# Attention's first loads, the fillers' weight loads and the last modulation load in another order

## The chip, the core and the metric

The kernel runs on one core of a Trainium2 chip. The time is the device time of one execution in microseconds (us), the median of several runs. The core has five engines with an instruction queue each: TensorE (PE) for matmuls, VectorE (DVE) and ScalarE (ACT) for elementwise work, GpSimd (POOL), and SyncE (SP), which here only issues DMAs. Each engine takes its instructions in the order in which they were written out. "Granted clock" is the share of TensorE's full clock that the chip's throttle allowed, as the profile records it.

## The reference

One layer of a Griffin-style block on x of 1024 tokens x 1024 channels, float32:

```python
sh1, sc1, g1, sh2, sc2, g2 = split(silu(c) @ ada_w + ada_b)       # six modulation vectors
h = rmsnorm(x, ln1_g) * (1.0 + sc1) + sh1
q, k, v, cb, cc, cx, ga, gb = split(h @ w_in)
q = rmsnorm(q, q_norm_g); k = rmsnorm(k, k_norm_g)                # 16 heads of 64
y_a = stick_breaking_attention(q, k, v)
y_b = cb * causal_dwconv(cc * cx, conv_w)                         # 3 taps
merged = sigmoid(ga) * (y_a @ w_branch_a) + sigmoid(gb) * (y_b @ w_branch_b)
x = x + g1 * (merged @ w_out)
h = rmsnorm(x, ln2_g) * (1.0 + sc2) + sh2
x = x + g2 * ((silu(h @ w_ffn_gate) * (h @ w_ffn_up)) @ w_ffn_down)
```

Stick-breaking attention weighs key s for query t > s by sigmoid(z_ts) times the product of (1 - sigmoid(z_tj)) over the keys j between them; there is no softmax.

## The kernel before

Matmuls run in a reduced float32 format at full rate, so every operand is split into a high and a low part (`whi`, `wlo`, `ath`, `atl`, `ya`'s two halves and so on): ACT copies the high part, DVE subtracts it from the original to get the low part, and three matmuls (high x high, high x low, low x high) make one product. The stages in order: modulation and norm, the projections, attention, branch a with its gates, W_out with the residual, the FFN.

**Attention** (`attention()`, from about 577 to 995 us in the trace) runs 16 heads x 8 query blocks of 128 queries, 128 steps. A step is: scores `z` on PE (L913, L914), sigmoid into `pt` on ACT (L915), the running product along the keys as one scan on DVE (L923; block i scans (i+1) x 128 elements), transposes `tr` on PE (L936, two steps later), the high copy `ath` on ACT (L939), the low part `atl` on DVE (L940), and every second step the product with the values, `o` on PE (L951, L952). Then ACT writes `otmp` (L956), DVE adds to `oy` (L958), and SP stores it to `d_ya` (L960). The scan form needs differences of neighbouring values: head pairs load `va` and `vb` (the values and the values one row on, 512 KB each, `load_v`, L844), `att_dv(h, 0)` subtracts them on DVE, and `att_dv(h, 1)` splits the difference into `vt` (ACT L855, DVE L136). L136 is the line of a helper that many DVE operations share. `att_load(h)` loads a head's q (`sqt`) and k (`skh`, `skl`), six DMAs on SP (L833 to L835).

**Fillers.** PE's own work in attention is less than that of DVE, so `fillers()` yields matmuls of other branches between attention's: for each of 8 column blocks m and two token halves n, cb = h @ w_cb (L1012 to L1014, into one of two `pj` banks), multiplied with a loaded tile of the convolution (`cy`, L1024, product L1030), split (`ybh` L1033, `ybl` L1034) and stored; later the same with w_b, and the gate product `mb` (L1062). The weight tile of an m is one load `raw<-w_cg` (L505) of 512 KB, split by ACT (L516) and DVE. n = 0 reads the h that is still in place; the first four k blocks of n = 1 have been stored to `d_h` and come back by two loads of 1 MB, hi and lo, into `big` (L1092). HEAD = 16 filler pieces are written out ahead of the first attention step.

**Branch a** loads attention's result back (`yr<-d_ya`, L1160, two buffers), splits it into `ya` (ACT L1164, DVE L136) and multiplies by w_a in the last heads and behind them; the gate's products `sgi` are L1184 (which frees PE's bank), L1185, L1190. Beside it `mods_last()` computes the last modulation vectors: it loads the raw c row broadcast to 128 partitions (`cab`, 512 KB, on POOL's queue, L1127), applies Silu (ACT L1128), and `mod_sums` loads 16 pieces of ada_w (`ad`, 512 KB each, three buffers, POOL's queue, L636) and reduces each with cab on DVE (L637).

**What sets the order.** The code is written in one order, and a scheduler places the instructions on each engine by its own estimate of times and by priority. `tc.issue_after(x)` holds the instructions written inside it until x has been placed, so that they don't move ahead of it; it adds no semaphore by itself. `lastld[0]` is the latest value load, `lastz[0]` the latest score matmul, `lastav[0]` the latest value product. DMAs of SP and ACT use eight semaphores in rotation, so a DMA issue also waits for the DMA that had its semaphore before.

Of the kernel before, what the change touches and what calls it, by code (L numbers as in the profile page):

```python
# [9 lines left out]
F32 = mybir.dt.float32  # L10
F32R = mybir.dt.float32r
AF = mybir.ActivationFunctionType
ALU = mybir.AluOpType
# [4 lines left out]
P = 128  # L18
T = 1024
D = 1024  # L20
KT = D // P
H = 16
DH = 64
# [7 lines left out]
def block_kernel(tc, x, x_t, cols, ada_1, ada_2, ada_row, w_q, w_kv, w_cg, w_a, w_b, w_o, w_g, w_u, w_d, out):  # L31
    nc = tc.nc
# [144 lines left out]
    cab = sp.tile([P, D], F32, name="cab")  # L177
# [648 lines left out]
    def att_load(h):  # L826
        pr, e0 = h // 2, (h % 2) * DH
        sqt = bp.tile([P, T], F32R, tag="sq", bufs=2, name=nm("sqt"))
        skh = bp.tile([P, T], F32R, tag="skh", bufs=2, name=nm("skh"))
        skl = bp.tile([P, T], F32R, tag="skl", bufs=2, name=nm("skl"))  # L830
        for e in range(2):
            es = slice(e * DH, (e + 1) * DH)
            nc.sync.dma_start(sqt[es].bitcast(F32), d_q[e][pr, e0:e0 + DH, :])  # L833
            nc.sync.dma_start(skh[es].rearrange("p (i t) -> p i t", t=P).bitcast(F32), d_k[0][pr // 4][:, e0:e0 + DH, pr % 4].rearrange("i p t -> p i t"))
            nc.sync.dma_start(skl[es].rearrange("p (i t) -> p i t", t=P).bitcast(F32), d_k[1][pr // 4][:, e0:e0 + DH, pr % 4].rearrange("i p t -> p i t"))  # L835
        hd[h] = (sqt, skh, skl)

    def load_v(h, e):
# [52 lines left out]
    lastav = [None]  # L891
    lastz = [None]
    lastld = [None]
    npt = [0]
    ats = {}
    ptof = {}
# [70 lines left out]
    def attention():  # L967

        steps = [(h, i) for h in range(H) for i in (LAST if h == H - 1 else ORDER)]
        for s in range(len(steps) + DAV):  # L970
            flush[0] = s >= len(steps)
            if s < len(steps):
                h, i = steps[s]
                if s % 8 == (0 if h else 3) and h + 1 < H:
                    with tc.issue_after(lastld[0].ins):
                        att_load(h + 1)
                with tc.issue_after(lastz[0].ins) if s else ExitStack():
                    if s in (1, 2):
                        att_dv(0, s - 1)
                    if s % 8 in ((4, 6) if h % 2 else (3, 5)) and h + 1 < H:  # L980
                        att_dv(h + 1, s % 8 // 5)
                    if s % 16 in (6, 7) and s + 16 < len(steps):
                        load_v(2 * (s // 16) + 2, 7 - s % 16)
                if s == 54:
                    with tc.issue_after(lastld[0].ins):
                        vl = load_vlast(1)
                if s == 56:
                    turn_vlast(1, vl)
                yield from att_scores(h, i)
            tr_ = att_trans(*steps[s - 2]) if 0 <= s - 2 < len(steps) else iter(())  # L990
            av_ = att_av(steps[s - DAV][0], steps[s - DAV][1] // 2) if s >= DAV and s % 2 != DAV % 2 else iter(())
            yield from itertools.islice(tr_, 1)
            if s >= DAV and steps[s - DAV][1] == 5:
                yield from av_
            yield from tr_
            if s < len(steps):
                att_scan(*steps[s])
            yield from av_

    def ps_f():  # L1000
# [15 lines left out]
    def fillers():  # L1016
        cb_w = {}
        for m, n in [(m + d, n) for m in range(0, KT, 2) for n in range(2) for d in range(2)]:
            if n == 0:
                with tc.issue_after(lastld[0].ins) if m > 1 else ExitStack():  # L1020
                    cb_w[m] = load_ch(w_cg[0, m])
            w = cb_w[m]
            y = fp.tile([P, 512], F32, tag="st", bufs=3, name=nm("cy"))
            nc.sync.dma_start(y, d_y[m, :, n * 512:(n + 1) * 512])  # L1024
            ps = ps_f()
            for kk in range(0, KT, KQ):
                if kk:
                    yield 0.65 * KQ
                mm_ch(ps, w, hh[n], hl[n], kk, kk + KQ)
            nc.vector.tensor_tensor(out=y, in0=ps, in1=y, op=ALU.mult)  # L1030
            yh = fq.tile([P, 512], F32R, tag="ybh", bufs=2, name=nm("ybh"))
            yl = fq.tile([P, 512], F32R, tag="ybl", bufs=2, name=nm("ybl"))
            nc.scalar.activation(yh, y, AF.Copy)  # L1033
            nc.vector.tensor_tensor(out=yl, in0=y, in1=yh.bitcast(F32), op=ALU.subtract)  # L1034
            nc.sync.dma_start(d_yb[0][n][:, m, :], yh.bitcast(F32))
            nc.sync.dma_start(d_yb[1][n][:, m, :], yl.bitcast(F32))
            yield 0.65 * KQ
        def load_sb(m, n):
            sb = fp.tile([P, 512], F32, tag="sgi", bufs=2, name=nm("sgi"))
            nc.sync.dma_start(sb, d_sgb[m, :, n * 512:(n + 1) * 512])  # L1040
            return sb

        sbs = [load_sb(m, 0) for m in range(2)]
        yh, yl = [], []
        for n in range(2):
            yh.append(big())
            yl.append(big())
            for k in range(0, KT, 2):
                nc.sync.dma_start(yh[n][:, k:k + 2].bitcast(F32), d_yb[0][n][:, k:k + 2])
                nc.sync.dma_start(yl[n][:, k:k + 2].bitcast(F32), d_yb[1][n][:, k:k + 2])  # L1050
        wb = {}
        for m, n in [(0, 0), (1, 0), (0, 1), (1, 1)] + [(m, n) for m in range(2, KT) for n in range(2)]:
            if n == 0:
                wb[m] = load_ch(w_b[m])
            sb = sbs.pop(0) if sbs else load_sb(m, n)
            ps = ps_f()
            for kk in range(0, KT, KQ):
                if kk:
                    yield 0.65 * KQ
                mm_ch(ps, wb[m], yh[n], yl[n], kk, kk + KQ)  # L1060
            mb = fp.tile([P, 512], F32, tag="st", bufs=3, name=nm("mb"))
            nc.vector.tensor_tensor(out=mb, in0=ps, in1=sb, op=ALU.mult)  # L1062
            nc.sync.dma_start(d_mb[m, :, n * 512:(n + 1) * 512], mb)
            yield 0.65 * KQ
# [16 lines left out]

    with tc.high_priority():
        att_load(0)
        for j in range(HEAD):
            next(fl)
            if j == 1:
                vl = load_vlast(0)
                turn_vlast(0, vl)
                load_v(0, 1)
                load_v(0, 0)  # L1090
                for e in range(2):
                    nc.sync.dma_start((hh, hl)[e][1][:, :4].bitcast(F32), d_h[e])  # L1092
    at_ = attention()
    flush, nfl = [0], 0
    pe, mine = len(nc.cur_bb.bb.instructions), set()
# [27 lines left out]
    def mods_last():  # L1123

        cab = mlp.tile([P, D], F32, name="cab3")
        with tc.issue_after(lastav[0].ins):
            nc.gpsimd.dma_start(cab, ada_row[0:1, :].broadcast_to([P, D]))  # L1127
            nc.scalar.activation(cab, cab, AF.Silu)  # L1128
        yield
        yield from mod_sums((3, 5), lambda i: mlp.tile([P, D], F32, tag="ad", bufs=3, name=nm("ad")),  # L1130
                            lambda s, t_: mlp.tile(s, F32, tag=t_, bufs=1, name=nm(t_)), cab, nc.gpsimd,
# [600 lines left out]
```

## Time and profile before

| | us |
|---|---|
| median of 3 runs (lowest, highest) | 1819.37 (1817.88, 1820.55) |
| the profiled execution's own time | 1820.9 |
| its span, first to last instruction | 1819.1 |
| PE busy | 1793.0 (99%) |
| DVE, ACT, POOL busy | 1358.5, 807.5, 369.8 |
| mean granted clock | 0.994 |

How to read the lines of the profile: in a timeline row stand the start, the duration, the engine, the line, the operation, output<-inputs, the shapes, how many instructions were merged (x2), and in brackets how long the engine had been idle ahead of it and what ended that wait. SPq is SP's queue; its rows are issues of DMAs, not their transfers. In the waits view the three numbers are the total, the number of waits and the longest. In the windows view stand, behind the window's length, each engine's busy time, then the granted clock, the share of the DMA engines and the rate in GB/s. PE is busy in nearly all of the span, so an engine that is late shows as a short PE wait.

### The profile page before, as it was taken

Reading aid. Unit: us, or ns where it says so; the run is one execution under the profiler, and the core shown is the slowest. Engines: PE = TensorE matmul, PEld = TensorE weight load, DVE = VectorE, ACT = ScalarE, POOL = GpSimd, SP = SyncE. Lnnn points to the kernel's source line nnn. Section 1 sums busy time; section 2 is a strip of 40 time slices with the busy share of each in tenths; the row PEclk is TensorE's granted clock in tenths of the full one; section 3 lists DMA queues with packets and bytes.
Section 4 is the critical chain, followed back from the end, with each engine's and each line's share of the span. In section 5 each row is a group of like instructions: output and inputs, shape, how many; then the busy total and the mean of one; then the engine's idle time right before and its main releaser. Section 6 shows DMA issues by size and latency. Waiting matters only on the chain.

```text
span 1819.1 us, 24498 instructions
## 1 busy us (share of the span) xinstructions
PE 1793.0 (99%) x8599; PEld 1490.5 (82%) x8599; DVE 1358.5 (75%) x1980; ACT 807.5 (44%) x1509; POOL 369.8 (20%) x297
## 2 busy tenths in 40 slices
PE   8999999999999999999999999999999999999999
PEld 6888877888888788888887888877888888878887
DVE  5876586787774789999996764689877887644766
ACT  5534364333433567666674221754443444322321
POOL 0024234733331000000000100115434444200000
PEclk9999999999999999999999999999999999999999
DMA  9479654223545977796645866424443443299876
GB/s 381 160 240 384 239 171 139 87 99 118 206 141 168 260 184 209 218 306 165 171 130 164 283 207 205 134 90 181 163 151 139 151 178 147 112 355 326 283 228 224
DMA packets 165006, 359.06 MB, mean 197 GB/s; under 512 B 15538, under 2 KB 60938, under 8 KB 163732
## 3 DMA queue, kind: packets, MB, share of 16 engines
q1 hardware_dynamic: 128300, 289.65, 48.9%
q10 hardware_dynamic: 33096, 55.25, 8.5%
q0 software_dynamic: 3488, 12.59, 2.0%
q8 instruction: 69, 1.13, 0.3%
q14 instruction: 53, 0.43, 0.1%
HBM read 247.84 MB, written 109.62 MB: 197 GB/s over the span
## 4 chain that ended last, share of the span: by engine, by line
PE 84%; DVE 6%; DMA 5%; ACT 2%; issue 2%; SPq 0%; ACTq 0%; POOL 0%; DVEq 0%; POOLq 0%
PE pj L293 9%; PE pj L133 7%; PE pj L131 7%; PE pj L132 7%; PE e L131 7%; PE e L132 7%; PE e L133 6%; PE e L1560 4%; PE e L1561 4%; PE e L1562 4%; PE pj L1012 4%; PE pj L1013 4%; PE pj L1014 4%; PE tr L936 3%; PE o L952 2%; PE z L913 2%
## 5 line engine op out<-in xcount | busy, mean ns | idle before, releaser
L923 DVE TENSOR_TENSOR_SCAN pt<-pt,mk 128x128 f32<-128x128 f32 (+7 forms) x128 | 172.4, 1347 | 0.7 <-ACT pt L915 0.7
L131 PE MATMUL e<-big,whi 128*128 128x512 f32 x352 | 138.0, 392 | 2.1 <-ACT c L1460 2.0
L132 PE MATMUL e<-big,whi 128*128 128x512 f32 x352 | 137.7, 391 | 0.0
L293 PE MATMUL pj<-whi,big 128*128 128x512 f32 x448 | 133.8, 396 | 3.9 <-ACT big L262 3.9
L133 PE MATMUL e<-big,wlo 128*128 128x512 f32 x352 | 137.5, 391 | 0.0
L136 DVE TENSOR_TENSOR c<-e,c 128x512 f32<-128x512 f32 x138 | 92.9, 687 | 57.0 <-PE e L133 55.9
L136 DVE TENSOR_TENSOR c<-pj,c 128x512 f32<-128x512 f32 x140 | 93.2, 682 | 45.5 <-PE pj L133 45.2
L131 PE MATMUL pj<-big,whi 128*128 128x512 f32 x320 | 125.0, 391 | 0.0
L133 PE MATMUL pj<-big,wlo 128*128 128x512 f32 x320 | 124.8, 390 | 0.0
L132 PE MATMUL pj<-big,whi 128*128 128x512 f32 x320 | 124.6, 389 | 0.0
L1560 PE MATMUL e<-whi,f 128*128 128x512 f32 (+1 forms) x319 | 121.8, 382 | 1.5 <-DMA f<-d_f 1.5
L1561 PE MATMUL e<-wlo,f 128*128 128x512 f32 (+1 forms) x319 | 121.8, 382 | 0.0
L1562 PE MATMUL e<-whi,f 128*128 128x512 f32 (+1 forms) x319 | 121.6, 382 | 0.0
L915 ACT ACTIVATE pt<-z,rq 128x512 f32<-128x512 f32 (+1 forms) x192 | 105.2, 576 | 23.3 <-PE z L914 22.8
L1012 PE MATMUL pj<-big,whi 128*128 128x512 f32 x256 | 114.3, 447 | 0.0
L136 POOL TENSOR_TENSOR ws<-raw,raw 128x512 f32<-128x512 f32 x40 | 54.5, 1362 | 275.8 <-DMA raw<-w_cg 127.7
L940 DVE TENSOR_TENSOR atl<-tr,ath 128x512 fp32r<-128x512 f32 (+1 forms) x192 | 102.8, 549 | 9.7 <-ACT ath L939 7.9
L939 ACT ACTIVATE ath<-tr 128x512 fp32r<-128x512 f32 (+1 forms) x192 | 93.1, 488 | 29.8 <-PE tr L936 28.9
L132 PE MATMUL e<-rl,whi 128*128 128x512 f32 x264 | 103.6, 392 | 2.5 <-DVE rl L136 2.5
L131 PE MATMUL e<-rh,whi 128*128 128x512 f32 x264 | 103.3, 391 | 0.2 <-ACT rh L1238 0.2
L133 PE MATMUL e<-rh,wlo 128*128 128x512 f32 x264 | 103.4, 392 | 0.0
L293 PEld LDWEIGHTS pj<-whi,big 128*128 128x128 f32 x448 | 84.9, 190 | 22.3 <-ACT big L262 4.7
(288 smaller groups left out, 4771.9 us busy)
## 6 DMA issues: line engine op xcount, KB each, us to landing
f<-d_f SPq DMA_DIRECT2D x77, 512.0 KB, 4.8
d_f<-fs SPq DMA_DIRECT2D x70, 512.0 KB, 3.6
raw<-w_cg SPq DMA_DIRECT2D x40, 512.0 KB, 4.2
raw<-w_u SPq DMA_DIRECT2D x26, 512.0 KB, 3.2
raw<-w_g SPq DMA_DIRECT2D x25, 512.0 KB, 3.6
raw<-w_kv SPq DMA_DIRECT2D x20, 512.0 KB, 5.9
ld<-ada SPq DMA_DIRECT2D x16, 512.0 KB, 7.0
d_t<-ts SPq DMA_DIRECT2D x16, 512.0 KB, 6.7
```

The lines of the kernel that those rows point to most:

```text
L131: nc.tensor.matmul(ps, wh[:, k, :], fh[:, k, :], start=(k == 0), stop=False)
L132: nc.tensor.matmul(ps, wh[:, k, :], fl[:, k, :], start=False, stop=False)
L133: nc.tensor.matmul(ps, wl[:, k, :], fh[:, k, :], start=False, stop=(k == 3))
L136: eng.tensor_tensor(out=out, in0=a, in1=b, op=op)
L293: nc.tensor.matmul(ps, a, b, start=(k == 0 and q == 0), stop=(k == KT - 1 and q == 2))
L915: nc.scalar.activation(pt[:, off + s0:off + s0 + m], z[:, :m], AF.Sigmoid, scale=rq[:, 1, i, h:h + 1])
L923: nc.vector.tensor_tensor_scan(out=pt[:, rev], data0=pt[:, rev], data1=mk[:, rev], initial=1.0, op0=ALU.mult, op1=ALU.max)
L940: nc.vector.tensor_tensor(out=tl[:, :nb, c0:c0 + P], in0=src, in1=th[:, :nb, c0:c0 + P].bitcast(F32), op=ALU.subtract)
L1012: nc.tensor.matmul(ps, wh, rh_, start=(k == 0), stop=False)
L1560: nc.tensor.matmul(o, sh, w[0][:, c], start=(j == 0), stop=False)
L1561: nc.tensor.matmul(o, sh, w[1][:, c], start=False, stop=False)
L1562: nc.tensor.matmul(o, sl, w[0][:, c], start=False, stop=(j == NJ - 1))
```

## The change

Four things move; no computation is added but one small product.

1. Head 0's q and k are loaded first (`att_load(0)`), then the two loads of h, held behind the last k load; head 0's values are held behind the first h load.
2. `att_dv(0, 0)` and `att_dv(0, 1)`, the value difference of head 0 and its split, are written behind the scan of their step instead of ahead of its scores.
3. The fillers' weight loads for m > 1 are held behind head 0's last k load instead of behind the latest value load.
4. `cab` is held behind a new small product on POOL, `mark`, that reads the last low half of `ya`; before, it was held behind the latest value product. The Silu is no longer held.

```diff
-            nc.sync.dma_start(skl[es].rearrange(...).bitcast(F32), d_k[1]...)
+            lastk[0] = nc.sync.dma_start(skl[es].rearrange(...).bitcast(F32), d_k[1]...)
...
                 with tc.issue_after(lastz[0].ins) if s else ExitStack():
-                    if s in (1, 2):
-                        att_dv(0, s - 1)
...
             if s < len(steps):
                 att_scan(*steps[s])
+            if s in (1, 2):
+                att_dv(0, s - 1)
             yield from av_
...
             if n == 0:
-                with tc.issue_after(lastld[0].ins) if m > 1 else ExitStack():
+                with tc.issue_after(first_k.ins) if m > 1 else ExitStack():
                     cb_w[m] = load_ch(w_cg[0, m])
...
         att_load(0)
+        first_k = lastk[0]
+        with tc.issue_after(first_k.ins):
+            for e in range(2):
+                first_h = nc.sync.dma_start((hh, hl)[e][1][:, :4].bitcast(F32), d_h[e])
         for j in range(HEAD):
             next(fl)
             if j == 1:
                 vl = load_vlast(0)
                 turn_vlast(0, vl)
-                load_v(0, 1)
-                load_v(0, 0)
-                for e in range(2):
-                    nc.sync.dma_start((hh, hl)[e][1][:, :4].bitcast(F32), d_h[e])
+                with tc.issue_after(first_h.ins):
+                    load_v(0, 1)
+                    load_v(0, 0)
...
         cab = mlp.tile([P, D], F32, name="cab3")
-        with tc.issue_after(lastav[0].ins):
+        mark = mlp.tile([P, 8], F32, name="mark")
+        behind = nc.gpsimd.tensor_tensor(out=mark, in0=yal[1][KT - 1][:, :8].bitcast(F32), in1=nhalf, op=ALU.mult)
+        with tc.issue_after(behind.ins):
             nc.gpsimd.dma_start(cab, ada_row[0:1, :].broadcast_to([P, D]))
-            nc.scalar.activation(cab, cab, AF.Silu)
+        nc.scalar.activation(cab, cab, AF.Silu)
```

What this does to the queues. The numbers behind the names only tell tiles apart, and behind the change lines from L891 on are one to six higher.

SP at the start of attention (sqt, skh, skl_5119 to 5121 are head 0's q and k; big_144 and big_146 take h; va, vb the values). Before:

```order
L1092 DMA big_146<-d_h_88 128x2048
L1092 DMA big_144<-d_h_87 128x2048
L833 DMA sqt_5119<-d_q_63 64x1024
L834 DMA skh_5120<-d_k_65 64x8x128
L835 DMA skl_5121<-d_k_66 64x8x128
L833 DMA sqt_5119<-d_q_64 64x1024
L834 DMA skh_5120<-d_k_65 64x8x128
L835 DMA skl_5121<-d_k_66 64x8x128
L1024 DMA cy_5138<-d_y 128x512
L861 DMA vl_5115<-d_v_0_67 8x4x128
```

And now:

```order
L833 DMA sqt_5119<-d_q_63 64x1024
L834 DMA skh_5120<-d_k_65 64x8x128
L835 DMA skl_5121<-d_k_66 64x8x128
L833 DMA sqt_5119<-d_q_64 64x1024
L834 DMA skh_5120<-d_k_65 64x8x128
L835 DMA skl_5121<-d_k_66 64x8x128
L1088 DMA big_144<-d_h_87 128x2048
L1088 DMA big_146<-d_h_88 128x2048
L1025 DMA cy_5140<-d_y 128x512
L861 DMA vl_5115<-d_v_0_67 8x4x128
```

The two h loads go from ahead of the six loads of q and k to behind them; cy, vl and then va and vb (which follow in both) keep their order.

DVE at the same place (pt_5110, 5111, 5112 are the scans of blocks 0, 1, 2; vb<-vb,va is the value difference, vt its split). Before:

```order
L1030 TENSOR_TENSOR cy_5138<-pj_5140,cy_5138 128x512
L1034 TENSOR_TENSOR ybl_5185<-cy_5138,ybh_5184 128x512
L923 SCALAR_TENSOR_TENSOR pt_5110<-pt_5110,mk 128x128
L876 TENSOR_TENSOR vlast<-vlast,tr_5149 64x64
L136 TENSOR_TENSOR vb_5161<-vb_5161,va_5118 128x8x64
L923 SCALAR_TENSOR_TENSOR pt_5111<-pt_5111,mk 128x256
L136 TENSOR_TENSOR vt_5251<-vb_5161,vt_5251 128x8x64
L940 TENSOR_TENSOR atl_5117<-tr_5261,ath_5116 128x128
L923 SCALAR_TENSOR_TENSOR pt_5112<-pt_5112,mk 128x384
```

And now:

```order
L924 SCALAR_TENSOR_TENSOR pt_5110<-pt_5110,mk 128x128
L1031 TENSOR_TENSOR cy_5140<-pj_5142,cy_5140 128x512
L876 TENSOR_TENSOR vlast<-vlast,tr_5151 64x64
L1035 TENSOR_TENSOR ybl_5185<-cy_5140,ybh_5184 128x512
L924 SCALAR_TENSOR_TENSOR pt_5111<-pt_5111,mk 128x256
L136 TENSOR_TENSOR vb_5163<-vb_5163,va_5118 128x8x64
L941 TENSOR_TENSOR atl_5117<-tr_5258,ath_5116 128x128
L924 SCALAR_TENSOR_TENSOR pt_5112<-pt_5112,mk 128x384
L136 TENSOR_TENSOR vt_5263<-vb_5163,vt_5263 128x8x64
```

The scan of block 1 moved ahead of the value difference, and the first scan moved ahead of cy's product and ybl.

SP, the weight load of m = 4 (raw_6227). Before it stands behind the values of heads 4 and 5:

```order
L844 DMA va_5935<-d_v_0_67 128x1024
L1035 DMA d_yb_69<-ybh_5889 128x512
L960 DMA d_ya_73<-oy_5902 64x256
L844 DMA vb_5982<-d_v_0_67 128x1024
L505 DMA raw_6227<-w_cg 128x1024
L1036 DMA d_yb_71<-ybl_5890 128x512
```

Now it stands ahead of head 3's q and k (sqt_5721, skh_5722):

```order
L1025 DMA cy_5744<-d_y 128x512
L505 DMA raw_6227<-w_cg 128x1024
L961 DMA d_ya_74<-oy_5473 64x256
L505 DMA raw_6391<-w_cg 128x1024
L1036 DMA d_yb_70<-ybh_5523 128x512
L1037 DMA d_yb_72<-ybl_5524 128x512
L961 DMA d_ya_74<-oy_5554 64x256
L1025 DMA cy_5918<-d_y 128x512
L961 DMA d_ya_73<-oy_5612 64x256
L834 DMA skh_5722<-d_k_65 64x8x128
L833 DMA sqt_5721<-d_q_63 64x1024
```

The same load stood in row 192 of SP's queue and stands in row 169. On POOL, cab stood directly ahead of the 16 ad loads; now three ad loads come first, then mark, then cab. On ACT the Silu moved from ahead of the last head's otmp to behind the second product's copy (L1189); on DVE the first two L637 moved from behind the second L1184 to behind the second L1190; on SP the last yr load moved ahead of a gate load and a weight load.

More of the change, by code (lines that the diff above doesn't have):

```diff
@@ L834, in att_load @@
             nc.sync.dma_start(skh[es].rearrange("p (i t) -> p i t", t=P).bitcast(F32), d_k[0][pr // 4][:, e0:e0 + DH, pr % 4].rearrange("i p t -> p i t"))
[L835 removed]
+            lastk[0] = nc.sync.dma_start(skl[es].rearrange("p (i t) -> p i t", t=P).bitcast(F32), d_k[1][pr // 4][:, e0:e0 + DH, pr % 4].rearrange("i p t -> p i t"))
         hd[h] = (sqt, skh, skl)
@@ L893, in block_kernel @@
     lastld = [None]
+    lastk = [None]
     npt = [0]
```

## The prediction

> **What bounds the kernel now.** I read the page first, then the waits of TensorE (PE), the timeline around each long wait, and the windows view for the granted clock.
>
> ```profile
> span 1819.1 us, 24498 instructions
> PE 1793.0 (99%) x8599; PEld 1490.5 (82%) x8599; DVE 1358.5 (75%) x1980; ACT 807.5 (44%) x1509; POOL 369.8 (20%) x297
> PE tr L936 <- DVE pt L923: 3.7, 8, 1.4
> ```
>
> PE is busy 1793.0 of 1819.1 us, so only 26.1 us of idle time, and what an idle PE does to its clock, can be won without removing a matmul, and the change removes none. In the waits (total, times, longest) attention's transposes stand for VectorE's scans with 3.7 us in 8 waits. PE's timeline places the three waits of attention that the change can reach; two of them are for ScalarE's (ACT's) copy of the transposed weights:
>
> ```profile
> 603.65 0.44 PE L936 MATMUL tr<-dm,pt 128*128 128x128 f32 x2 [1.42 <-DVE pt L923]
> 667.39 0.39 PE L951 MATMUL o<-ath,vt 128*128 128x256 f32 x1 [1.23 <-ACT ath L939]
> 668.11 0.39 PE L952 MATMUL o<-atl,vt 128*128 128x256 f32 x1 [0.34 <-DVE atl L940]
> 988.20 0.38 PE L951 MATMUL o<-ath,vt 128*128 128x256 f32 x1 [1.90 <-ACT ath L939]
> 989.63 0.58 PE L952 MATMUL o<-atl,vt 128*128 128x256 f32 x1 [0.36 <-DVE atl L940]
> ```
>
> I call them A (603.65, 1.42 us), B (667.39, 1.23 + 0.34) and C (988.20, 1.90 + 0.36). In the windows view the column behind POOL's busy time is the granted clock, then come DMA share and GB/s:
>
> ```profile
> 604.00:620.00 16.00, 15.61 (x91) 12.89 (x91) 15.88 (x23) 11.81 (x27) 0.00 (x0) 1.00 1.05 341
> 668.00:672.00 4.00, 3.89 (x17) 3.70 (x18) 4.00 (x6) 1.67 (x5) 0.00 (x0) 0.57 1.11 179
> 989.00:993.00 4.00, 3.64 (x14) 3.04 (x13) 1.74 (x3) 1.20 (x2) 0.00 (x0) 0.57 0.78 242
> ```
>
> Behind A the clock stays at 1.00. Behind B and C it is 0.57 for 4 us, which costs 4 x (1 - 0.57) = 1.7 us each. So A is worth 1.4 us, B 1.57 + 1.7 = 3.3 us, C 2.26 + 1.7 = 4.0 us. The Trainium skill ("TensorE: Matmul & The Clock Gate", Part 1: The HAM clock gate) has the clock fall only after an idle window of about 3.4 us; by that rule B and C, at most 2.3 us each, would cost no clock and the sum below would be smaller by 3.4 us. The two rows at 0.57 speak against it, and I go by the rows.
>
> **Part 1, the start of attention (A).** What stands there on VectorE (DVE), SyncE (SP) and PE:
>
> ```profile
> 596.77 0.69 DVE L1030 TENSOR_TENSOR cy<-pj,cy 128x512 f32<-128x512 f32 x1 [7.37 <-DMA cy<-d_y]
> 599.56 0.42 DVE L923 TENSOR_TENSOR_SCAN pt<-pt,mk 128x128 f32<-128x128 f32 x1 [0.71 <-ACT pt L915]
> 602.30 0.69 DVE L136 TENSOR_TENSOR vb<-vb,va 128x512 f32<-128x512 f32 x1 [2.21 <-DMA vb<-d_v]
> 602.91 0.68 DVE L923 TENSOR_TENSOR_SCAN pt<-pt,mk 128x256 f32<-128x256 f32 x1
> 604.50 0.95 DVE L923 TENSOR_TENSOR_SCAN pt<-pt,mk 128x384 f32<-128x384 f32 x1
> 600.65 0.95 ACT L915 ACTIVATE pt<-z,rq 128x256 f32<-128x256 f32 x2 [0.91 <-PE z L914]
> 577.00 0.80 SPq L1092 DMA_DIRECT2D big<-d_h  x2
> 590.43 0.57 SPq L835 DMA_DIRECT2D skl<-d_k  x1
> 594.27 1.08 SPq L844 DMA_DIRECT2D vb<-d_v  x1
> 599.41 0.50 PE L1012 MATMUL pj<-big,whi 128*128 128x512 f32 x1
> 605.59 0.52 PE L936 MATMUL tr<-dm,pt 128*128 128x128 f32 x3 [0.16 <-DVE pt L923]
> ```
>
> A is the value difference: DVE, which works in order, waits 2.21 us for vb with the scan of 256 queued behind. The change puts that scan ahead of the difference, and the wait at 603.65 goes. Three things are late next.
>
> First, the new DVE order also puts cy's product (which frees one of the two pj banks) behind the first scan. It ran at 596.77; now it ends at 599.56 + 0.42 + 0.69 = 600.67 at the earliest. The filler matmul at 599.41 needs that bank: a new PE wait of 1.26 us in place of the 1.42. The scores behind it come 1.26 us later too: the pt of 256, done at about 601.1 (the first of the two from 600.65), at 602.4, its scan of 0.68 at 603.0. There the difference can start, if vb is in. In before 3.15 us lay between the difference's start at 602.30 and the end of scan 384 (604.50 + 0.95 = 605.45), the scan of 256 among them; without its 0.68 they are 2.5 us, so scan 384 ends at 605.5 and the transposes for which PE waited at 605.59 come as they came. Net so far: 0.0 us.
>
> Second, the values. The d_h loads (2 x 1 MB) went at 577.00, into an empty queue; now they follow head 0's last k load (590.43 before; 590 to 591 now, since the two ahead of it move up but still wait for earlier transfers), so they go at about 591 to 593, with cy, va and vb behind them in one queue.
>
> ```profile
> 588.00:597.00 9.00, 9.00 (x42) 7.44 (x41) 1.52 (x3) 1.23 (x3) 0.00 (x0) 1.00 0.84 249
> big<-d_h SPq DMA_DIRECT2D x2, 1024.0 KB, 7.5
> ```
>
> h then lands at 598.5 to 600.5 by its 7.5 us, and PE first reads it at 599.41, which is now 600.67 anyway: covered by the new wait. The DMA share in this stretch was 0.84, so 9 x 0.16 = 1.4 us is free, and the last k load, now earlier, frees perhaps 1.5 us more, against 2 MB / 379 GB/s (the rate of 982 to 988, quoted below) = 5.5 us that h needs. vb landed at 602.3 by its row; I take 1 us later than the 603.0 allowed above, with 0 (all fits in) and 3 us (5.5 - 2.9, rounded up) as ends: +1.0.
>
> Third, DVE's 1.38 us of cy and ybl (two of 0.69) ran before in idle time (7.37 us idle ahead of cy) and now lie in a stretch (604 to 620, above) where DVE is busy 15.88 of 16 us. PE, 15.61 of 16, already waits there; lag between 0 and 1.38, I take a little under the middle: +0.6. Sum of part 1: **+1.6 us**, from -1.4 (A goes and nothing follows) to +5.
>
> **Part 2, the fillers' weight loads (B).** SP's and ACT's rows:
>
> ```profile
> 658.12 0.49 SPq L844 DMA_DIRECT2D vb<-d_v  x1
> 658.66 1.50 SPq L505 DMA_DIRECT2D raw<-w_cg  x1
> 665.64 0.63 ACT L516 ACTIVATE whi<-raw 128x512 fp32r<-128x512 f32 x1 [3.33 <-DMA raw<-w_cg]
> ```
>
> The load goes right behind vb, lands 7 us later, and ACT waits 3.33 us for it with the copy that PE needs queued behind. Gated by head 0's k instead, it stands 23 rows earlier in SP's queue, ahead of head 3's q and k loads instead of head 4's, so about a head earlier: some 25 us, with 16 heads between 599 and 990. Its buffer is free by then. The ACT wait goes, and with it PE's 1.57 us and the clock: **-3.3 us**. At worst DVE (wlo, then atl) is late next and half stays (-1.6). The earlier loads for m = 2, 3 and 6, 7 replace loads that nobody on PE waited for: 0.
>
> **Part 3, the modulation load (C).** POOL, ACT and SP:
>
> ```profile
> 969.72 0.77 POOL L1127 DMA_DIRECT2D cab<-ada_row  x1 [406.70 <-ACT ath L939]
> 975.19 0.63 ACT L1164 ACTIVATE ya<-yr 128x512 fp32r<-128x512 f32 x1 [4.33 <-DMA yr<-d_ya]
> 970.69 6.21 SPq L1160 DMA_DIRECT2D yr<-d_ya  x3
> 979.74 0.63 ACT L1164 ACTIVATE ya<-yr 128x512 fp32r<-128x512 f32 x1 [1.99 <-DMA yr<-d_ya]
> 978.61 0.39 SPq L1160 DMA_DIRECT2D yr<-d_ya  x1
> 987.03 0.63 ACT L1164 ACTIVATE ya<-yr 128x512 fp32r<-128x512 f32 x1 [6.17 <-DMA yr<-d_ya]
> 987.56 0.58 ACT L939 ACTIVATE ath<-tr 128x512 fp32r<-128x512 f32 x1
> 982.00:988.00 6.00, 4.29 (x23) 3.32 (x22) 0.31 (x1) 0.97 (x2) 1.05 (x2) 1.00 1.02 379
> ```
>
> C is ACT standing 6.17 us at a yr tile, the copy for PE right behind. That yr went at 978.61, waiting for one of two buffers, and the chain that frees them begins with the ya at 975.19, whose yr was issued at 970.69 and met cab's broadcast (issued 969.72). Without cab, that yr should take what the third of this row took: issued 0.32 ahead of the row's end at 976.90, so at 976.6, and in at 979.74, 3.2 us. It then lands at 973.9 instead of 975.19, the chain moves up 1.3 us, and the yr of 978.61 goes at 977.3. With its old 8.4 us it lands at 985.7 and ath is done at 986.9, where PE arrives at 986.3: most of the wait gone. Issued earlier it also gets ahead of the ad loads that fill 982 to 988 at 379 GB/s, and lands sooner. I take all of C: **-4.0 us**; the ends are -0 and -4.0.
>
> Afterwards cab comes late. Its issue now waits for the last ya difference, then its Silu, then two L637 on DVE, and only behind these, in DVE's order, the product L1184 that frees the bank for PE:
>
> ```profile
> 1005.64 0.69 DVE L136 TENSOR_TENSOR ya<-yr,ya 128x512 fp32r<-128x512 f32 x1 [2.84 <-ACT ya L1164]
> 993.72 1.06 ACT L1128 ACTIVATE cab<-cab 128x1024 f32<-128x1024 f32 x1
> 1006.85 1.21 DVE L637 CUSTOM_DVE_ANT_0 ad<-ad,cab 128x1024 f32<-128x1024 f32 x1
> 1013.78 0.39 PE L1012 MATMUL pj<-ya,whi 128*128 128x512 f32 x1
> ad<-ada POOLq DMA_DIRECT2D x16, 512.0 KB, 6.0
> ```
>
> PE needs the bank at 1013.78, or 1009.8 with C gone. The last ya then moves up with PE, and by 1 to 2 us more since its yr is issued ahead of two loads: about 1001. Add 0.7 for the ya, 0.7 for the multiplication on POOL, the landing, 1.06, 2 x 1.2 and 0.7: 1009.8 with a landing like yr's 3.2 us, 1012.6 with ad's 6.0. POOL's next ad stands behind cab, so cab has little beside it and is nearer to the first: **+0.5 us** (0 to 8.7, below).
>
> **Sum:** 1.6 - 3.3 - 4.0 + 0.5 = -5.2 us. The profiled run took 1820.9 us around its span of 1819.1; it lies 1.5 above the median of 1819.37, and I take the difference from the median: **1814.2 us**.
>
> **The rivals.** *C stays:* DMA is as full at 982 to 988 by the other loads, cab or no cab, and yr lands no earlier. For it: the ad loads are not moved. Against: yr gets 1.3 us ahead of them. 1.6 - 3.3 = -1.7: 1817.7 (the late cab has its old slack then).
>
> *B only moves:* DVE, then PE, waits a little later for the same split: for it, DVE is 4.00 of 4 us busy at 668 to 672. -1.6 kept instead of -3.3: 1815.9.
>
> *The loads pile up at the start:* cy behind 2 MB of h lands at 604 instead of 597. PE waits 599.41 to 604.8, with the clock drop 5.4 + 1.7, less the 1.42 of A: +5.7 instead of +1.6: 1818.3. It decides when cy lands behind 601.
>
> *The clock drops anyway:* if the 0.57 behind B and C has another cause than these waits, it stays, and B and C return 3.8 us instead of 7.3: -5.2 + 3.4 = -1.8: 1817.6. For it: A's 1.42 us had no drop. Against: both drops stand right behind the two longest stalls of attention. (By the rule of the Trainium skill named above, waits this short are no cause.)
>
> *Slower: cab is too late.* If the last ya stays at 1005.64 while PE comes 4 us earlier: 1006.3 + 0.7 + 6.0 + 1.06 + 2.4 + 0.7 = 1017.2, against PE at 1009.8: 7.4 us, with the clock 9.1, and less what overlaps about 8.7. Then 1.6 - 3.3 - 4.0 + 8.7 = +3.0: 1822.4. It decides from a cab that lands behind 1007 in PE's earlier time. Against it: yr stands earlier in SP's queue.
>
> **How the numbers follow.** Chances: forecast 0.46, C stays 0.18, B only moves 0.08, pile-up 0.12, clock anyway 0.05, cab too late 0.11. The range: all gains with A gone give -1.4 - 3.3 - 4.0 = -8.7, so 1810.7; upwards it reaches past the pile-up and C staying to 1820.5 and leaves out cab too late. 0.2% (3.6 us, below 1815.7 or above 1823.0) is what a measurement of this kernel can tell. Most of the forecast (0.42), and the rivals where other terms come out better than taken (0.12), lie below 1815.7: faster 0.54. Slower than 1823.0 are only the worse part of cab too late and two rivals at once: 0.08. The rest lies within: 0.38.
>
> **What would show it.** Right: no PE wait for pt at the second transposes but one of about 1.3 us at a filler matmul ahead of them, behind cy's product; no ACT wait for raw near 665 and clock 1.00 behind it; no 6 us ACT wait for yr, and clock 1.00 behind the last heads. Wrong: a PE wait on big<-d_h or cy over 2 us; the same 1.90 us at the last head; PE waiting for L1184 behind L637.

## The result and the profile after

The changed kernel took 1824.58 us (median of 8 runs, 1820.91 to 1827.81), the kernel before 1819.11 us beside it (8 runs, 1815.09 to 1820.72). The ratio is 1.0032 with a 95% interval of 1.0023 to 1.0041: slower by 0.32%, about 5.8 us, where 5.2 us faster was forecast and the range ended at 1820.5. The profiled execution took 1824.49 us around a span of 1822.7.

The changed kernel's page, in its first line:

```profile
span 1822.7 us, 24508 instructions
```

The waits of PE (total, times, longest):

```profile
PE pj L1013 <- DVE sgi L1190: 4.1, 2, 2.3
PE tr L870 <- DMA vl<-d_v: 3.0, 1, 3.0
PE tr L937 <- DVE pt L924: 2.9, 8, 0.9
PE z L914 <- ACT pt L916: 2.7, 3, 1.9
```

In the list before stood:

```profile
PE o L951 <- ACT ath L939: 3.1, 2, 1.9
```

These two waits for ath, one in B and one in C, were forecast to go and are gone. Three new entries stand in their place: for vl, for pt (L916), and for the gate product sgi. To see what each place is worth I measured stretches between the same DVE instructions in every profile: the scan of step 0, of step 16, of step 26, of the last step 127, and the last split of a gate product in branch a. Their starts:

| | scan 0 | scan 16 | scan 26 | scan 127 | last gate split | span |
|---|---|---|---|---|---|---|
| before | 599.56 | 647.31 | 677.07 | 971.40 | 1085.36 | 1819.1 |
| changed | 600.05 | 654.41 | 681.46 | 975.18 | 1090.46 | 1822.7 |

So the start of attention (A) costs 54.36 instead of 47.75 us, +6.6. The stretch with B takes 27.05 instead of 29.76, and 0.6 us more is won up to scan 127: -3.3. (That 0.6 is not the change's: all other profiles of the table below, with the old weight loads too, take as long there as the changed kernel.) The stretch with C and branch a takes 115.28 instead of 113.96: +1.3. With 0.5 ahead of attention and -1.5 in all that follows this is the 3.6 us between the spans. The other 1.8 us to the medians is that the kernel before was profiled in a run of 1820.9, above its median.

**A.** SP's queue in the timeline:

```profile
574.58 0.47 SPq L833 DMA_DIRECT2D sqt<-d_q  x1
585.09 0.57 SPq L834 DMA_DIRECT2D skh<-d_k  x1
589.27 0.57 SPq L835 DMA_DIRECT2D skl<-d_k  x1
590.63 3.31 SPq L1088 DMA_DIRECT2D big<-d_h  x2
593.99 0.43 SPq L1025 DMA_DIRECT2D cy<-d_y  x1
594.52 0.56 SPq L861 DMA_DIRECT2D vl<-d_v  x1
595.87 1.49 SPq L844 DMA_DIRECT2D vb<-d_v  x1
```

The longest of SP's waits between 574 and 600:

```profile
SPq L834 <- DMA d_sga<-c: 10.0, 1, 10.0
```

Head 0's q goes earlier, but the first k load waits 10.0 us for a store to d_sga, and the whole queue waits with it. The load doesn't touch that data; I put the wait down to the eight semaphores that the DMAs take in turn, which no run tried by itself. So h, once at 577.00, goes at 590.63 to 593.9. The windows (granted clock, DMA share and GB/s at the end) show what became of the place that h left, first before, then now:

```profile
577.00:588.00 11.00, 11.00 (x50) 9.09 (x49) 5.16 (x8) 2.98 (x6) 0.00 (x0) 1.00 0.95 296
577.00:588.00 11.00, 11.00 (x51) 9.09 (x50) 5.16 (x8) 2.49 (x5) 0.00 (x0) 1.00 0.15 50
```

The DMA engines, busy at 0.95 before, stand nearly idle at 0.15 for 11 us. The windows behind it, in the changed kernel:

```profile
594.00:602.00 8.00, 5.62 (x27) 4.54 (x25) 0.42 (x1) 0.37 (x1) 0.00 (x0) 1.00 1.00 377
602.00:609.00 7.00, 6.18 (x28) 4.81 (x28) 2.71 (x5) 1.80 (x4) 0.00 (x0) 0.76 1.12 193
```

DVE, ACT and PE in the timeline:

```profile
602.30 0.69 DVE L1031 TENSOR_TENSOR cy<-pj,cy 128x512 f32<-128x512 f32 x1 [1.83 <-DMA cy<-d_y]
608.58 0.69 DVE L136 TENSOR_TENSOR vb<-vb,va 128x512 f32<-128x512 f32 x1 [2.22 <-DMA vb<-d_v]
609.30 0.63 ACT L855 ACTIVATE vt<-vb 128x512 fp32r<-128x512 f32 x1 [2.92 <-DVE vb L136]
602.59 0.42 PE L870 MATMUL tr<-dm,vl 9*64 9x9 f32 x8 [2.97 <-DMA vl<-d_v]
610.73 0.33 PE L914 MATMUL z<-skh,sqt 128*128 128x128 f32 x1 [1.92 <-ACT pt L916]
```

The DMA engines are at share 1.00 and 377 GB/s for 8 us: 3 MB, two thirds of it h. cy (256 KB) and vl (some KB) land behind it at 602.3 to 602.6 (cy's product ran at 596.77 before), and PE waits 2.97 us for vl. vb lands at 608.6, where it was 602.3 before. The difference now stands behind the second scan, so that scan doesn't wait; but ACT's split of the difference (L855) has the next pt queued behind it, and PE waits 1.92 us for that pt. The granted clock in 602 to 609 is 0.76: another 1.7 us.

**B** went as forecast. At the place where the clock had been 0.57, PE is busy all the time at 1.00 (first row). The second row is the window where C had its drop, the third a new place, in branch a:

```profile
667.00:672.00 5.00, 5.00 (x32) 4.26 (x31) 4.95 (x6) 3.84 (x10) 0.00 (x0) 1.00 0.84 273
989.00:993.00 4.00, 4.00 (x26) 3.52 (x25) 1.12 (x2) 0.63 (x1) 0.00 (x0) 1.00 0.90 303
1016.00:1020.00 4.00, 4.00 (x12) 3.09 (x12) 4.00 (x7) 1.15 (x2) 0.53 (x1) 0.57 0.96 309
```

**C** went too, and was given back: no wait for ath is left, the row of 989 has its clock at 1.00, and ACT's longest wait for a yr between 975 and 990 is 2.88 us (first row below), where it was 6.17. ACT, then POOL, ACT, DVE and PE in branch a, in the timeline:

```profile
986.87 0.63 ACT L1170 ACTIVATE ya<-yr 128x512 fp32r<-128x512 f32 x1 [2.88 <-DMA yr<-d_ya]
1005.35 0.57 POOL L1133 DMA_DIRECT2D cab<-ada_row  x1
1011.57 1.06 ACT L1134 ACTIVATE cab<-cab 128x1024 f32<-128x1024 f32 x1 [3.17 <-DMA cab<-ada_row]
1012.67 1.23 DVE L637 CUSTOM_DVE_ANT_0 ad<-ad,cab 128x1024 f32<-128x1024 f32 x1 [4.84 <-ACT cab L1134]
1015.80 0.51 PE L1013 MATMUL pj<-ya,whi 128*128 128x512 f32 x1 [2.29 <-DVE sgi L1190]
1029.52 0.69 DVE L1190 TENSOR_TENSOR sgi<-pj,sgi 128x512 f32<-128x512 f32 x1 [4.83 <-DMA sgi<-d_sga]
1030.35 0.47 PE L1013 MATMUL pj<-ya,whi 128*128 128x512 f32 x1 [1.78 <-DVE sgi L1190]
```

PE was ready at 1015.80 - 2.29 = 1013.51; it started on this product at 1013.78 before, though the last scan now starts 3.8 us later: that is C's 4 us. But cab takes 6.2 us from its issue to its Silu, DVE stands 4.84 us at the first L637 with the gate product queued behind, and PE waits 2.29 us and loses 1.7 us of clock (the row of 1016). Then DVE waits 4.83 us for a gate load (two buffers, each freed by a product that now comes late), and PE 1.78 us more. Together 5.8 us against C's 4.0 in these two profiles.

### The profile page after: what moved, and what is told of

It is laid out like the page before. It is cut to its first block, busy times and chain, and to the rows that moved or that the text cites. A ratio compares the mean times of both kernels' runs of the same rounds, so it can differ in the third digit from the quotient of the medians.

```text
span 1822.7 us, 24508 instructions
## 1 busy us (share of the span) xinstructions
PE 1791.7 (98%) x8599; PEld 1488.9 (82%) x8599; DVE 1356.6 (74%) x1980; ACT 807.7 (44%) x1509; POOL 369.5 (20%) x298
## 4 chain that ended last, share of the span: by engine, by line
PE 82%; DVE 7%; DMA 6%; ACT 3%; issue 2%; POOL 1%; ACTq 0%; SPq 0%; DVEq 0%; POOLq 0%
PE pj L293 9%; PE e L131 6%; PE e L133 6%; PE e L132 6%; PE pj L131 6%; PE pj L133 6%; PE pj L132 6%; PE e L1567 4%; PE e L1566 4%; PE e L1568 4%; PE pj L1013 3%; PE pj L1015 3%; PE pj L1014 3%; PE tr L937 3%; PE o L953 2%
## 5 line engine op out<-in xcount | busy, mean ns | idle before, releaser
L916 ACT ACTIVATE pt<-z,rq 128x512 f32<-128x512 f32 (+1 forms) x192 | 105.0, 576 | 31.1 <-PE z L915 30.6
L636 POOL DMA_DIRECT2D ad<-ada x16 | 8.7, 544 | 466.0 <-ACT ath L940 418.0
```

What stands on the lines that cost most here:

```text
L916: nc.scalar.activation(pt[:, off + s0:off + s0 + m], z[:, :m], AF.Sigmoid, scale=rq[:, 1, i, h:h + 1])
```

## Experiments

The theory: each place belongs to one part of the change. A is lost because 2 MB of h stand ahead of cy, vl, va and vb in one queue; B and C are won; the late cab loses more than C wins. Its rivals stand in the expectations, word for word as recorded before each run. All stretches in one table, in us (A from scan 0, B from 16, then from 26, and C with branch a from 127 to the last gate split):

| kernel | 0 to 16 | 16 to 26 | 26 to 127 | 127 on | ratio to before (95%) |
|---|---|---|---|---|---|
| before | 47.75 | 29.76 | 294.33 | 113.96 | |
| changed | 54.36 | 27.05 | 293.72 | 115.28 | 1.0032 (1.0023, 1.0041) |
| e1_raws | 48.44 | 27.07 | 293.71 | 111.93 | 0.9986 (0.9978, 0.9995) |
| e2_cab | 49.02 | 28.66 | 293.77 | 115.10 | 1.0016 (1.0008, 1.0025) |
| e3_loads | 53.35 | 29.50 | 293.78 | 114.44 | 1.0021 (1.0009, 1.0033) |
| e4_dv | 47.18 | 28.25 | 293.74 | 110.62 | 0.9994 (0.9984, 1.0005) |
| f1_no_loads | 46.82 | 27.06 | 293.79 | 116.60 | 0.9998 (0.9988, 1.0007) |
| f2_vl_first | 52.91 | 27.05 | 293.80 | 118.15 | 1.0034 (1.0022, 1.0046) |
| f3_cab_mid | 48.11 | 27.06 | 293.78 | 114.67 | 0.9994 (0.9983, 1.0005) |
| f4_no_cab | 46.73 | 27.06 | 293.78 | 109.71 | 0.9986 (0.9977, 0.9994) |
| h1_h_last | 58.92 | 27.06 | 293.74 | 114.36 | 1.0080 (1.0065, 1.0094) |
| h2_sums_late | 47.47 | 27.07 | 293.70 | 107.50 | 0.9973 (0.9963, 0.9982) |
| k1_cab_early | 47.30 | 27.05 | 293.77 | 114.06 | 0.9992 (0.9979, 1.0004) |
| k2_sums_late | 47.52 | 27.06 | 293.81 | 111.05 | 0.9956 (0.9944, 0.9969) |

The kernels e1 to e4 were measured on one chip, f1 to f4 on a second, h1 and h2 on a third, k1 and k2 on a fourth, each time with the kernel before beside them. h2 and k2 are one kernel: its ratios lie 3.1 us apart and its last stretches 3.55 us (107.50 and 111.05). So a difference of 1 to 3 us between two chips, or between two single profiles in the last column of stretches, decides nothing.

### e1, the weight loads alone

```diff
-                with tc.issue_after(lastld[0].ins) if m > 1 else ExitStack():
+                with tc.issue_after(first_k.ins) if m > 1 else ExitStack():
```

> Only the fillers' weight loads are gated by head 0's last k load; all else as before. Theory (four places, each owned by one part of the change): the ACT wait for raw near 665 goes, PE's 1.23 + 0.34 us go, the granted clock behind it is 1.00, and the time falls by 3.3 us (ratio 0.9982). Rival (DVE is late next and keeps half): -1.6 us, with a PE wait for atl of some 0.8 us at the same place.

Ratio 0.9986: -2.5 us (-4.0 to -0.9). The interval holds both -3.3 and the rival's -1.6; the profile decides. Both waits of B are gone and none for atl of 0.3 us or more is left; every kernel with this edit takes 27.05 to 27.07 us there, those without 28.25 to 29.76. The theory holds. The price of 3.3 us was that of one execution at the dear end: in e4, which has the loads as before, the wait for ath at this place was absent from the profile and the stretch only 1.2 us longer.

### e2, cab alone

```diff
-        with tc.issue_after(lastav[0].ins):
+        behind = nc.gpsimd.tensor_tensor(out=mark, in0=yal[1][KT - 1][:, :8].bitcast(F32), in1=nhalf, op=ALU.mult)
+        with tc.issue_after(behind.ins):
             nc.gpsimd.dma_start(cab, ada_row[0:1, :].broadcast_to([P, D]))
```

> Only cab's load is moved behind the last ya difference; all else as before. Theory: the 1.90 us wait at 988 goes with its clock loss (-4.1 us), and PE waits about 2.3 us behind L637 with 1.7 us of clock (+4.0): sum 0 +- 1 us. Rival (in the changed kernel the wait at 988 went only because PE came there 3.8 us later, by the losses at the start of attention): here PE is not late, the wait for ath at 988 stays at 1.5 us or more, and the time is 3 to 4 us above before.

Ratio 1.0016: +2.9 us (1.5 to 4.5). The wait at 988 is gone although PE wasn't late, so the rival falls. The time is nearer to the rival's all the same, for other reasons: my sum of 0 left out the second wait, of 1.86 us, for the gate load, and priced C by one dear execution (see Part 3 below). Moving cab alone makes this kernel slower.

### e3, the order of the loads alone

```diff
         att_load(0)
+        first_k = lastk[0]
+        with tc.issue_after(first_k.ins):
+            for e in range(2):
+                first_h = nc.sync.dma_start((hh, hl)[e][1][:, :4].bitcast(F32), d_h[e])
...
-                load_v(0, 1)
-                load_v(0, 0)
-                for e in range(2):
-                    nc.sync.dma_start((hh, hl)[e][1][:, :4].bitcast(F32), d_h[e])
+                with tc.issue_after(first_h.ins):
+                    load_v(0, 1)
+                    load_v(0, 0)
```

> Only the order of the loads is changed (q and k, then h, then the values); the value difference stays ahead of the second scan, the fillers' weight loads and cab as before. Theory (2 MB of h ahead of cy, vl, va and vb in one queue make all of them late): vl lands near 602, vb near 608, PE waits about 3 us for vl and then for the scan behind the value difference; +7 to +10 us. Rival (the loss needs the new DVE order of the value difference and its split): at most +3 us.

Ratio 1.0021: +3.8 us (1.6 to 6.0), below the 7 to 10 expected and above the rival's bound of 3, though the interval reaches below it. PE's timeline decides for the theory's mechanism:

```profile
601.54 0.40 PE L870 MATMUL tr<-dm,vl 9*64 9x9 f32 x8 [3.46 <-DMA vl<-d_b]
```

The stretch is 53.35 us, against 47.75, 48.44 and 49.02 in the three profiles with before's code there: +4.9 on their mean. So the loss doesn't need the new DVE order. I had overpriced it, in part by what A itself costs: PE's wait at the second transposes, 1.42 to 2.58 us in those three profiles, is 0.92 us here. And vb was not as late as expected: its difference ran at 605.83, not near 608.

### e4, the value difference alone

```diff
-                    if s in (1, 2):
-                        att_dv(0, s - 1)
...
                 att_scan(*steps[s])
+            if s in (1, 2):
+                att_dv(0, s - 1)
```

> Only the value difference of head 0 is written behind the scan; loads as before. Theory: PE's 1.42 us wait at 603.65 goes and little follows: -1.4 to 0 us, the next wait (tr x3) at most 0.5 us. Rival (the order on DVE itself costs): 0 to +2 us, with a longer wait for the third scan.

Ratio 0.9994: -1.1 us (-2.9 to +0.9). No wait is left at the second transposes, and the stretch takes 47.18 us. The ratio can't tell the theory from no change; the profile shows no cost. The four parts alone add up to -2.5 + 2.9 + 3.8 - 1.1 = 3.1 us against the 5.8 of the whole change, a gap that lies within their intervals.

### f1, all but the order of the loads

The changed kernel with e3's edit taken back.

> The whole change but for the order of the loads (h goes first, as before; value difference behind the scan, fillers' weight loads gated early, cab behind the last ya). Theory (the loss at the start of attention is the order of the loads alone, and the parts add up as they measured alone: -2.5 + 2.9 - 1.1): -0.7 us against before, within 2 us, 5 to 7 us below the changed kernel. Rival (the new DVE order shares in the loss once the loads are early): +2 us or more.

Ratio 0.9998: -0.4 us (-2.2 to +1.3), as expected. Without the new order of the loads the change costs nothing net, so that order is worth 1.0032 - 0.9998, or 6.2 us (6.5 against f2 on the same chip). What is left nearly cancels: the gain of B against the loss by cab. Cab's two losses are there, with 2.31 and 3.69 us.

### f2, vl ahead of h

```diff
         with tc.issue_after(first_k.ins):
+            vl = load_vlast(0)
             for e in range(2):
```

> The changed kernel with the small loads of vl ahead of h instead of behind it. Theory (2 MB of h delay everything behind them, vl was only the first to be waited for): the 3 us wait for vl turns into one for cy's product of about the same length, vb still lands near 608, and the time is that of the changed kernel within 1.5 us. Rival (the small vl loads alone hold PE): 3 us or more below the changed kernel.

Ratio 1.0034, as the changed kernel. PE's first wait changes its name and hardly its length, as the theory has it:

```profile
601.53 0.50 PE L1013 MATMUL pj<-big,whi 128*128 128x512 f32 x1 [2.81 <-DVE cy L1031]
613.74 0.50 PE L914 MATMUL z<-skh,sqt 128*128 128x512 f32 x1 [2.12 <-ACT pt L916]
```

One thing missed: vb didn't land near 608; its difference ran at 604.22 without a wait, and the loss was the same. So what costs here is cy or vl behind h, more than vb.

### h1, h behind the values

```diff
-                with tc.issue_after(first_h.ins):
+                with tc.issue_after(first_k.ins):
                     load_v(0, 1)
                     load_v(0, 0)
+                with tc.issue_after(lastld[0].ins):
+                    for e in range(2):
+                        nc.sync.dma_start((hh, hl)[e][1][:, :4].bitcast(F32), d_h[e])
```

> The changed kernel, but with head 0's values right behind its q and k, and the two h loads behind them (they come to stand behind head 1's q and k too). Theory (whatever stands behind the others in this queue pays, since q and k leave only at 585 to 590 and 2 MB don't fit in between): vb lands near 601 and no scan waits for it, but PE now waits 6 to 9 us for h at the first filler of the second half; the time is 0 to 4 us above the changed kernel. Rival (only the values are urgent, h has time): 4 us or more below the changed kernel.

Ratio 1.0080: +14.5 us (11.8 to 17.1), 8.7 above the changed kernel. The rival falls, and the theory's own price was too low:

```profile
609.22 0.77 PE L1013 MATMUL pj<-big,whi 128*128 128x512 f32 x1 [9.48 <-DMA big<-d_h]
611.56 0.80 PE L1014 MATMUL pj<-big,whi 128*128 128x512 f32 x1 [1.58 <-DMA big<-d_h]
```

No scan waits for vb any more, and h is late instead. Of the three orders tried behind the k loads (h first, vl ahead of h, h last) none is good (52.9 to 58.9 us up to scan 16); the kernels that send h near 577, into the idle time, take 46.7 to 49.0.

### f3, cab behind an earlier ya, and f4, cab as before

Both are f1 but for this line; f4 has before's lines for cab.

```diff
-        behind = nc.gpsimd.tensor_tensor(out=mark, in0=yal[1][KT - 1][:, :8].bitcast(F32), in1=nhalf, op=ALU.mult)
+        behind = nc.gpsimd.tensor_tensor(out=mark, in0=yal[1][4][:, :8].bitcast(F32), in1=nhalf, op=ALU.mult)
```

> As f1 (loads as before), but cab waits for the fifth ya of the second half instead of the last. Theory (cab is only too late there): the 2.3 us wait behind L637 is gone or under 0.5 us, the wait near 988 stays away, and the time is 5 us below before and 4 us or more below f1. Rival (the wait at 988 was moved by cab's transfer wherever it is put, or L637 itself costs): no more than 2 us below f1.

> As f1, but cab as before (behind the latest value product): only the value difference and the fillers' weight loads are changed. Theory: -2.5 - 1.1 = -3.6 us against before; the wait near 988 is there (0.8 to 2.1 us). It is then 2 to 4 us above f3. Rival (moving cab gains nothing at 988): equal to f3 within 1 us.

f3 took 0.9994 (-1.1 us) and f4 0.9986 (-2.5 us). For f4 the theory's -3.6 lies within the interval (-4.2 to -1.1). For f3 it missed: f3 should have been 4 us or more below f1 and 2 to 4 below f4; it is 0.7 below f1, as its rival said, and 1.4 above f4. In f3 the waits at 988 and for cab are gone, but DVE and PE show what came instead:

```profile
1000.08 0.69 DVE L136 TENSOR_TENSOR ya<-yr,ya 128x512 fp32r<-128x512 f32 x1 [2.05 <-ACT ya L1168]
1001.29 1.21 DVE L637 CUSTOM_DVE_ANT_0 ad<-ad,cab 128x1024 f32<-128x1024 f32 x1
1013.38 0.69 DVE L1188 TENSOR_TENSOR sgi<-pj,sgi 128x512 f32<-128x512 f32 x1 [3.58 <-DMA sgi<-d_sga]
1014.13 0.50 PE L1013 MATMUL pj<-ya,whi 128*128 128x512 f32 x1 [1.66 <-DVE sgi L1188]
```

The last ya starts 1000.08 - 967.65 = 32.4 us behind the last scan (1004.42 - 975.18 = 29.2 in the changed kernel): cab, issued at 989.38, now travels beside the last yr, which I take for the cause. Behind it DVE works through L637 ahead of the gate products, and a gate load comes late. So I now thought that not only cab's lateness mattered, but that the sums stand ahead of the gate products whose buffers set the pace; h2 tests it.

### h2, the sums later

f1, with the sums L637 starting three gate products later:

```diff
-        for _ in range(1 + m % 2):
+        for _ in range(0 if it < 3 else 2):
```

> As f1 (loads as before, cab behind the last ya), but the modulation sums L637 begin three gate products later. Theory (with cab there, the first loss is L637 standing ahead of the gate product that frees PE's bank): the first wait for sgi near 1008 (2.3 us and its clock) is gone, the second, which is for the gate load, stays at 1 to 3.5 us; 2 to 4 us below f1. Rival (ACT waiting for cab with the weight split behind it holds PE just as long): within 1 us of f1.

Ratio 0.9973: -4.9 us (-6.7 to -3.3), 4.5 below f1. No wait for sgi is left, none for ath, and the stretch takes 107.50 us against f1's 116.60, with no PE wait of 0.3 us in it. The first loss was L637 ahead of the gate product. The second wait, which the theory expected to stay, went with it, so it had followed from the first; the kernel's second profile (k2) has 0.6 us of it.

### k1 and k2, cab early and late beside each other

k1 is h2 with cab's load where before has it; k2 is h2 again. k1's edit against h2:

```diff
-        mark = mlp.tile([P, 8], F32, name="mark")
-        behind = nc.gpsimd.tensor_tensor(out=mark, in0=yal[1][KT - 1][:, :8].bitcast(F32), in1=nhalf, op=ALU.mult)
-        with tc.issue_after(behind.ins):
+        with tc.issue_after(lastav[0].ins):
             nc.gpsimd.dma_start(cab, ada_row[0:1, :].broadcast_to([P, D]))
-        nc.scalar.activation(cab, cab, AF.Silu)
+            nc.scalar.activation(cab, cab, AF.Silu)
...
     ml = mods_last()
+    next(ml)
```

The added line writes cab's load out ahead of the loop that the sums now start late in.

> As h2 (sums L637 three gate products later, loads as before, value difference and weight loads changed), but cab's load is where it was before the change. Theory (moving cab gains the wait at 988, and only the sums gave it back): the wait for ath near 982 to 988 is there again (0.7 to 2.1 us, in some executions with 1.7 us of clock), and the time is 1 to 4 us above k2. Rival (the late sums alone made the gain of h2): within 1 us of k2.

> The kernel of h2 again, beside k1 on one chip. Theory: 4 to 6 us below before, 1 to 4 us below k1. Rival: equal to k1 within 1 us.

k1 took 0.9992 (-1.5 us), k2 0.9956 (-8.0 us; h2, the same kernel, 0.9973). The two stand 6.5 us apart, more than expected but on the theory's side. k1's profile has C back, with a clock loss:

```profile
983.27 0.38 PE L952 MATMUL o<-ath,vt 128*128 128x256 f32 x1 [2.06 <-ACT ath L940]
```

The window behind it:

```profile
984.00:989.00 5.00, 4.63 (x16) 3.71 (x15) 1.95 (x4) 2.55 (x3) 0.00 (x0) 0.53 0.70 224
```

k2's waits of PE hold neither:

```profile
PE tr L937 <- DVE pt L924: 3.9, 8, 1.1
PE pj L1013 <- DVE sgi L1188: 0.6, 1, 0.6
```

So the late cab is worth its C only with the sums out of the way. Nor do the late sums win alone: with cab early, k1 (late sums, 0.9992) shows no gain on f4 (sums as before, 0.9986, on another chip), while late cab and late sums together took 0.9973 and 0.9956. h2, measured twice, took the least of all here: loads as before, the value difference behind the scan, weight loads gated early, cab late, sums later.

## Why the prediction was wrong, point by point

One row of the kernel before that the first point needs, the window just ahead of vb's landing:

```profile
597.00:602.30 5.30, 5.23 (x32) 4.08 (x30) 1.69 (x5) 2.15 (x5) 0.00 (x0) 1.00 1.06 230
```

- **Part 1, the values (+1.0, ends 0 and 3).** This step failed: that h, sent behind the k loads, would hardly delay the loads behind it. I let 2.9 of h's 5.5 us lie in free DMA time. The share of 0.84 was that of 588 to 597; behind 597 the engines were full in before too (1.06, in the row above), so what was free came too early for the loads that are waited for. cy came 5.5 us later (602.30 against 596.77) and vb 6.3 (608.58 against 602.30), all of h's 5.5 or a little more; in e3's and f2's profiles vb lost less. I also summed cy only as a product in DVE's order, with its load on time, and vl not at all: vl, some KB in the same queue, was what PE waited for first, and ACT's split of the difference, with a pt behind it, was the second way in. Part 1 came to +6.6 instead of +1.6, beyond its end of +5. The mechanism was in the rival of the piled-up loads, with 0.12 and +5.7: its sign (cy behind 601) was met, at 602.3, though PE's wait was for vl.
- **Part 1, the scan.** The wait at the second transposes went, as forecast. In its place I expected 1.3 us behind cy's product; it was 2.97 us for vl. e4 and f1 show that moving the value difference costs nothing. In both, cy's product still stands ahead of the first scan, so that part of the new DVE order came with the loads, and the +0.6 for it was not measured by itself.
- **Part 2 (-3.3).** Right in mechanism; the size fits these two profiles, in part by luck of the draw. e1's ratio says -2.5, and the profiles with the old loads take 1.2 (e4) to 2.7 us (before) more than 27.06. e3 has before's waits (1.21 and 0.34 us) without a clock drop, and its way from scan 16 to scan 127 is only 0.8 us shorter than before's: the drop cost less than the 1.7 us that I gave it.
- **Part 3, C (-4.0).** Right in mechanism: in all profiles with cab moved the wait was gone, in all with cab early it was there, with 0.69 to 2.12 us for ath. The size was that of a dear execution. Over the six profiles with cab early the waits for ath and atl come to 1.85 us on the mean and three had a clock drop: some 2.7 us with 1.7 for each drop, an estimate.
- **Part 3, the late cab (+0.5, ends 0 and 8.7).** This step failed too. The place was right (the product behind L637), the size wrong. I took a landing near yr's 3.2 us, as POOL had nothing beside it; from issue to Silu it took 6.2 us, near the 6.0 of the ad loads. And the wait for the gate load behind it was in no term. Measured 2.29 + 1.7 + 1.78 = 5.8 us. The rival of the late cab had +8.7 by another reason, a last ya that stays; it moved up with PE as I had forecast. Part 3 as a whole was to win 3.5 us. By e2's ratio it cost 2.9; the last stretch takes 115.9 us on the mean of the five profiles with cab behind the last ya, and 112.1 on that of the five with cab early, with the sums in their old place in all ten.
- **The sum.** A and the late cab were 5 us each too low; either alone would have left about "no change". I gave "two rivals at once" next to no chance though they have no cause in common. The rivals that kept the drops at B and C, the wait of C, or half of B all fell: the clock is 1.00 where the waits went, and no wait for atl stayed at B.
- **The clock.** The row decided rightly against the rule of the Trainium skill ("TensorE: Matmul & The Clock Gate", Part 1: The HAM clock gate) that it falls behind an idle window of about 3.4 us: it fell to 0.57 behind 2.29 us here. But it does not fall behind every such wait (below).

## What to carry to other kernels

A load that leaves an idle slot for the place ahead of an urgent one can cost the urgent one its whole transfer time (here 2 MB cost cy 5.5 us); ask what was free where it stood, up to the landing of the last transfer that is waited for, and count every small load in the queue. "First in the queue" is first only if the one at the head can go: here it waited 10 us for a store that it didn't need. A wait removed from the bottleneck is time that the next stage must be able to take; look for what stands in order ahead of the product that frees its buffers, and move that too.

## What the runs showed of the hardware

The granted clock fell behind some short waits of PE and not behind others of the same length. In e2, two waits in PE's timeline:

```profile
603.83 0.48 PE L936 MATMUL tr<-dm,pt 128*128 128x128 f32 x2 [2.58 <-DVE pt L923]
1011.58 0.47 PE L1012 MATMUL pj<-ya,whi 128*128 128x512 f32 x1 [2.47 <-DVE sgi L1186]
```

The windows behind them:

```profile
603.80:608.80 5.00, 4.97 (x21) 4.33 (x22) 4.62 (x8) 3.15 (x9) 0.00 (x0) 0.66 1.04 323
1011.60:1016.60 5.00, 5.00 (x22) 4.16 (x23) 4.88 (x9) 1.15 (x2) 0.76 (x3) 1.00 0.93 315
```

2.58 us cost 1.7 us of clock, 2.47 us cost none. Take all PE waits of 1.2 us or more in attention and branch a over the fourteen profiles, but for one that came right behind another in h1, with the clock still down. Of the 20 up to 2.6 us, 7 were followed by a granted clock of 0.60 to 0.68 over the next 5 us and 13 by 1.00; all 7 from 2.78 us up were followed by 0.50 to 0.71. So a wait of some 2 us costs on average about 0.6 us more than its length, with a large spread, and one profile shows one case: C was priced at 4.0 us from an execution with a drop, and in e3's profile the same wait (1.70 us) came without one. Why one falls and another doesn't was not tried.
